# Three moves in a hand-written TensorE order: second gate row behind the first row's copies, first row later, state products one step behind the turned keys

## The chip, the cores and the metric

The kernel runs on one core of a Trainium2 chip, as one program in one launch. The metric is the device time of one execution in microseconds (us); less is better. The runs of one kernel differ by some tenths of a per cent, so a difference under about 0.5% of the time isn't told apart from none.

## What is computed

One inference step of a small diffusion backbone: 128 context tokens and 512 latent tokens (T = 640 together), width 1,024, two layers. Layer 0 (even) has four HGRN2 heads (state 128 x 128) and four GLA heads (state 64 x 128) that share one input projection; layer 1 (odd) has eight retention heads. Each head is a chunkwise gated linear scan in both directions:

```python
def even_mixer(h, s0_a, s0_b, lb, w_in, gk_w, gk_b, gn_w, w_out):
    p = h @ w_in
    aq, ai, af_f, af_b, ag, bq, bk, bv, bg, bl_f, bl_b = jnp.split(p, EVEN_SPLIT_IDX, axis=-1)
    ...
    o_a, st_a = bidir_scan(hd(jax.nn.silu(aq), H_A), (-jnp.expm1(lf_f), -jnp.expm1(lf_b)),
                           hd(ai, H_A), (lf_f, lf_b), s0_a)
    def gla_log_gate(low, d):
        return jax.nn.log_sigmoid((low @ gk_w[d] + gk_b[d]).astype(jnp.float32)) / GLA_GATE_NORM
    ...
    o = group_rms_norm(o, gn_w).astype(h.dtype) * jax.nn.silu(jnp.concatenate([ag, bg], axis=-1))
    return o @ w_out, st_a, st_b

# chunk_gated_linear, per direction:  S_t = diag(g_t) S_{t-1} + k_t v_t^T,  o_t = S_t^T q_t
```

Conditioning: shift, scale and gate of a layer are `SiLU(c) @ ada_w[l] + ada_b[l]`. The outputs are the normed tokens of both groups and the scan states of the context tokens.

## The kernel before, in words

**Matmuls.** Each float32 weight tile (128 x 512, 256 KB, loaded by SyncE in L171) is split in two parts: `wh` (a cast on ScalarE, L180) and the remainder `wl` (a subtraction on GpSimd, some on VectorE, L182). The activations are split likewise (`h0h`, `h0l`, `h1h`, `h1l` by token group; the groups are 256 and 384 columns). A projection with features on the partitions (`proj_fm`, PSUM tiles `pf`) has 8 steps over the 1,024 inputs ("k-steps") of 6 matmuls each, 48 in all; with tokens on the partitions (`proj_tm`) the tiles are called `pt`. The trace shows each of the small fp32 matmuls (`px`, `pkv`, `po`, `pada`, `pz`) as two records, so 16 matmuls of `pada` are "x32". All PSUM tiles share eight buffers in turn: a matmul that begins a new tile waits for whoever read the tile that had the buffer before.

**The order of TensorE is written by hand.** `run(gen)` walks through a projection, and after each k-step it looks whether the work in the queue `bg` is due by a clock that the program advances by estimated matmul lengths; if so, it lets that generator go on to its next `yield d`, which makes it due again `d` later. `low_bg` is a second queue: `ada_stream`, the conditioning of layer 0's gate and of layer 1, in 16 steps of 16 `pada` matmuls, each on four `araw` tiles of 256 KB (L281, four buffers in all, loaded by SyncE once the matmuls of the step before have freed them). `drain(left)` steps `bg` with no projection in between until `left` generators remain; while the one in front isn't due, it steps `low_bg` instead. The other engines' order (VectorE = DVE, ScalarE = ACT, GpSimd = POOL, SyncE = SP) follows from a scheduler of the framework; each engine runs its own list in order.

**GLA's rows.** The four GLA heads are two rows of two heads. `gla_gates(r)` (L746 to L767) makes a row's gates `T1` (in the code `g1`): 4 matmuls `pz`, absolute value (L755), ACT table loads, Exp and Ln (L757, L758), `T1 <- T1 - e` (L759, DVE), Exp (L762), Ln (L764), and on DVE L765 and L767. For each row the loop (L774 on) projects the queries (`use_bq`, copied by ACT, L779) and the keys (`use_bk`: one copy by DVE, L783, one by ACT, L784), multiplies Q = q x gate on POOL (`prepare`, L656 and L657) and puts the row's generator in `bg`.

**A row** (`row`, L659 on) computes the scores on the diagonal (`px` from q and K), then six levels, each: `kmix` (ACT, L687) gathers `km`, 20 matmuls `px` from Q and km, `merge` on DVE: K x gates (L695), Q x gates (L697), and the next level's gates (L699, half as long at each level); the scores are copied into A (L706, L714, L716 to L718). Then it turns the keys: 8 transposes `pkt` and two ACT copies `kt` (L725), `yield D_KT`; then the products `pkv` and the states S (DVE, L405 and L408), `yield D_KV`; then the outputs `po` (first v x A, then S x Q).

**HGRN's heads** (loop behind it): project q, `drain(1)` (the head before the last must be finished), project the two forget gates, then K (L819), T1 (L821), `ks` (POOL) and `prepare`, and the row goes into `bg` with a delay of 7.0. Behind the heads stand the decays of layer 1 and the gate projections (`pt`), which the last rows share.

Of the kernel before, what the change touches and what calls it, by code (L numbers as in the profile page):

```python
# [41 lines left out]
def hybrid_kernel(  # L42
# [20 lines left out]
    def ps(name="ps"):  # L63
        return psp.tile([128, 512], F32, tag="ps", name=name)

    def tokt(name):
        return tok.tile([128, D], F32, tag="tok", name=name)

    def t25(name):
        return misc.tile([128, T], F32, tag="t25", name=name, bufs=3)  # L70
# [9 lines left out]
    def mm(out, lhsT, rhs, share=1, **kw):  # L80
        n = 1
        for _, cnt in rhs.ap[1:]:
            n *= cnt
        clock[0] += (max(n, 256) / 2400.0 if lhsT.dtype == F32R else max(n, 128) / 600.0) / share
        PE.matmul(out, lhsT, rhs, **kw)  # L85
# [5 lines left out]
    def add_bg(gen, delay=0.0, queue=bg):  # L91
        queue.append([gen, clock[0] + delay])

    def step(queue):
        e, late = queue[0], len(deferred) if queue is bg else 0
        try:
            wait = next(e[0])
            e[1] = clock[0] + wait
        except StopIteration:
            queue.pop(0)  # L100
            return
        flush(late)
# [5 lines left out]
    def run(gen):  # L108
        for _ in gen:
            while bg and bg[0][1] <= clock[0]:  # L110
                step(bg)
            if low_bg and low_bg[0][1] <= clock[0]:
                step(low_bg)
# [60 lines left out]
    def weights(i, look=None):  # L174
        while made[0] <= min(i + (LOOK if look is None else look), len(specs) - 1):
            n = made[0]
            src = specs[n]
            raw, _ = raw_load(src)
            wh = wp.tile([128, 512], F32R, tag="wh", name="wh", bufs=8)
            S.copy(wh, raw)  # L180
            wl = wp.tile([128, 512], F32R, tag="wl", name="wl", bufs=8)
            (V if n in on_dve else G).tensor_tensor(wl, raw, wh.bitcast(F32), op=SUB)  # L182
            loaded[n] = tuple(w.rearrange("p (a b) -> p a b", a=src.shape[1]) for w in (wh, wl))
            made[0] += 1
        return loaded[i]
# [23 lines left out]
    def in_turn(sums, first, last):  # L209

        for n in range(3):
            for out, pairs in sums:
                mm(out, *pairs[n], start=first and n == 0, stop=last and n == 2)

    def proj_fm(ids, act, use):
        p = [ps("pf") for _ in GROUPS]
        for k in range(KC):
            wh, wl = (w[:, k % 4, :] for w in weights(ids[k // 4]))
            sums = []
            for g in (1, 0):  # L220
                hh, hl = (a[:, k, :] for a in act[g])
                sums.append((p[g][:, :GROUPS[g][1]], ((wh, hh), (wh, hl), (wl, hh))))
            in_turn(sums, k == 0, k == KC - 1)
            if k < 7:
                yield
        for g in (1, 0):
            use(g, p[g])
        yield
# [265 lines left out]
    def x_square(t):  # L494
        return rms(x_t[t], junk)
# [19 lines left out]
    with tc.manual_schedule(engines={mybir.EngineType.Activation, mybir.EngineType.DVE, mybir.EngineType.Pool}):  # L515
# [8 lines left out]
        r = [x_square(t) for t in range(2)]  # L524
# [129 lines left out]
    def prepare(Q, q, g1):  # L654

        G.tensor_tensor(Q[:, 0, :], q, g1[:, 0, :], op=MUL)  # L656
        G.tensor_tensor(Q[:, 1, :], q, g1[:, 1, :], op=MUL)  # L657
# [76 lines left out]
    def new_KQ():  # L734
        return tuple(rows.tile([128, 2, T], F32, tag=n, name=n, bufs=2) for n in "KQ")

    def new_q():
        return rows.tile([128, T], F32, tag="q", name="q", bufs=2)

    def new_g():  # L740
        return rows.tile([128, 2, T], F32, tag="T1", name="T1", bufs=2)
# [4 lines left out]
    def gla_gates(r):  # L746

        K, Q, q, g1 = gla[r]
        e = Q
        for d in range(2):  # L750
            b = vecs[:, O_GKB + 2 * d + r:O_GKB + 2 * d + r + 1]
            for g, (off, n) in enumerate(GROUPS):
                p = ps("pz")
                mm(p[:, :n], gkw[:, d, 128 * r:128 * r + 128], low[:, off:off + n], start=True, stop=True)
                S.activation(e[:, d, off:off + n], p[:, :n], AF.Abs, bias=b)  # L755
                V.tensor_scalar(g1[:, d, off:off + n], p[:, :n], b, 0.0, op0=ADD, op1=ALU.min)
        S.activation(e, e, AF.Exp, scale=-1.0)  # L757
        S.activation(e, e, AF.Ln, bias=1.0)  # L758
        V.tensor_tensor(g1, g1, e, op=SUB)  # L759
        y0 = [t25("y0") for d in range(2)]  # L760
        for d in range(2):
            S.activation(y0[d], g1[:, d, :], AF.Exp, scale=1.0 / 16.0)  # L762
        for d in range(2):
            S.activation(e[:, d, :], y0[d], AF.Ln, bias=tiny)  # L764
        V.scalar_tensor_tensor(e, g1, 1.0 / 16.0, e, op0=MUL, op1=SUB)  # L765
        for d in range(2):
            V.scalar_tensor_tensor(g1[:, d, :], e[:, d, :], 1.0, y0[d], op0=ADD, op1=MUL)  # L767

    gla_gates(0)
    gla_gates(1)  # L770
    y_t = [tokt(f"y{t}") for t in range(NT)]
    gn = tokt("gn")
    ACTQ.dma_start(gn, gn_even[0:1, :].to_broadcast([128, D]))
    for r in range(2):  # L774
        K, Q, q, g1 = gla[r]

        def use_bq(g, p, q=q):
            off, n = GROUPS[g]
            S.activation(q[:, off:off + n], p[:, :n], AF.Copy, scale=0.125)  # L779

        def use_bk(g, p, K=K):
            off, n = GROUPS[g]
            V.tensor_copy(K[:, 0, off:off + n], p[:, :n])  # L783
            S.copy(K[:, 1, off:off + n], p[:, :n])  # L784

        run(proj_fm(ids_b[r][0], act, use_bq))
        run(proj_fm(ids_b[r][1], act, use_bk))
        prepare(Q, q, g1)
        s0 = [state_gla[0, 0, d, 2 * r:2 * r + 2].rearrange("h k v -> (h k) v") for d in range(2)]
        cols = [512 + 256 * r, 640 + 256 * r]  # L790
        add_bg(row(q, g1, K, Q, (K[:, 0, :], 2.0), [(0, 64), (64, 128)], cols, cols, s0,
                   new_gla[0, 0, :, 2 * r:2 * r + 2].rearrange("d h k v -> (h k) d v"), y_t, gn), D_GLA)


    def v_use(t, p):
# [3 lines left out]
    for h in range(4):  # L799
        q = new_q()  # L800
# [7 lines left out]
        g1 = new_g()  # L808
# [9 lines left out]
        K, Q = new_KQ()  # L818
# [194 lines left out]
    for part in range(2):  # L1013
        p = ps("pt")
        for k in range(KC):
            wh, wl = weights(ids_o1[1][k])
            cols = slice(256 * part, 256 * part + 256)
# [3 lines left out]


DVE_FROM = 5
D_LEVEL, D_KT, D_KV, D_GLA, D_PREP, D_ROPE, D_TURN, D_ADA, D_RT, D_RV = 1.8, 0.5, 1.2, 7.0, 7.0, 11.0, 2.5, 7.0, 1.5, 1.5


# [42 lines left out]
```

## Time and profile before

| | before |
|---|---|
| runs | 795.43 us median of 3 (794.3 to 798.55) |
| the profiled execution | 797.16 us, span 795.4 us, granted clock 0.984 |
| TensorE (PE) | 758.2 us busy, 95% of the span |
| DVE, ACT, POOL | 428.8, 334.2 and 289.6 us busy (54%, 42%, 36%) |
| HBM | 86.31 MB read, 8.16 MB written, 119 GB/s over the span |

TensorE is the engine that is nearly always busy; the others have room on average, and matter where TensorE waits for one of them. The granted clock is given as a share of 2.4 GHz. Times within the program are microseconds from the start of the span. GLA's rows lie between 62 and 165 us, HGRN's heads between 165 and 335, and behind 390 us the rest of the program stands in the same order as after the change.

### The profile page before, as it was taken

How to read it: one execution, taken by the hardware profiler on the slowest of the kernel's cores; microseconds unless marked ns; L12 is line 12 of the kernel's file. 1: busy time of each engine (PE TensorE's matmuls, PEld its weight loads, DVE VectorE, ACT ScalarE, POOL GpSimd, SP SyncE). 2: the span in 40 equal slices, each digit the busy share in tenths (PEclk: the TensorE clock that was granted, in tenths of full speed). 3: DMA queues.
4: the chain of work that ended last, by engine and by line, in shares of the span. 5: the costliest groups of instructions: out<-in, count | busy, mean ns of one | idle time of the engine just before them, and what ended most of it. 6: DMA issues, size and time to landing. Idle time of an engine off the chain costs nothing.

```text
span 795.4 us, 15429 instructions
## 1 busy us (share of the span) xinstructions
PE 758.2 (95%) x6116; PEld 664.2 (84%) x6116; DVE 428.8 (54%) x744; ACT 334.2 (42%) x757; POOL 289.6 (36%) x263
## 2 busy tenths in 40 slices
PE   4999789999989899899999999999999999999996
PEld 3768778789889798778888888899999999888885
DVE  4973793752986666663444940036454646324433
ACT  6447643444534444443534552324333332235322
POOL 2261430265552522331344521544443532043221
PEclk9999899999999999999999999999999999999998
DMA  9982432364433431318524432334333333544003
GB/s 292 315 268 92 142 108 62 114 181 126 144 96 107 147 98 38 81 41 265 152 84 145 152 118 87 94 105 106 100 104 90 115 91 94 173 126 133 14 26 133
DMA packets 104776, 98.62 MB, mean 124 GB/s; under 512 B 7660, under 2 KB 80896, under 8 KB 104704
## 3 DMA queue, kind: packets, MB, share of 16 engines
q1 hardware_dynamic: 83520, 82.15, 33.4%
q10 hardware_dynamic: 21184, 15.49, 7.1%
q8 instruction: 48, 0.79, 0.4%
q14 instruction: 24, 0.20, 0.1%
HBM read 86.31 MB, written 8.16 MB: 119 GB/s over the span
## 4 chain that ended last, share of the span: by engine, by line
PE 68%; DVE 8%; issue 2%; ACT 1%; POOL 1%; DMA 1%; ACTq 0%; POOLq 0%; DVEq 0%
PE pt L85 32%; PE pf L85 21%; PE po L85 5%; PE px L85 4%; PE pkv L85 3%; DVE K L695 2%; DVE T L821 1%; DVE T L699 1%; PE pyt L89 1%; PE pada L85 1%; PE pkt L89 1%; DMA rot<-qk 1%; DVE K L819 1%; DVE Q L697 1%; PE pxt L89 1%
## 5 line engine op out<-in xcount | busy, mean ns | idle before, releaser
L182 POOL TENSOR_TENSOR wl<-raw,wh 128x512 fp32r<-128x512 f32 x142 | 203.0, 1444 | 309.4 <-ACT wh L180 264.4
L180 ACT CAST wh<-raw 128x512 fp32r<-128x512 f32 x168 | 103.2, 621 | 97.8 <-PE pf L85 37.0
L85 PE MATMUL pf<-h0h,wh 128*128 128x384 f32 (+1 forms) x256 | 64.1, 332 | 0.0
L335 DVE SCALAR_TENSOR_TENSOR y<-po,rr,gn 128x128 f32<-128x128 f32 x80 | 24.2, 345 | 72.3 <-POOL rr L158 60.5
L85 PE MATMUL pf<-h1h,wh 128*128 128x384 f32 (+1 forms) x256 | 60.3, 317 | 0.0
L85 PE MATMUL pf<-h0l,wh 128*128 128x384 f32 (+1 forms) x256 | 58.9, 311 | 0.0
L85 PE MATMUL pf<-h0h,wl 128*128 128x384 f32 (+1 forms) x256 | 58.6, 310 | 0.0
L85 PE MATMUL pf<-h1l,wh 128*128 128x384 f32 (+1 forms) x256 | 58.3, 309 | 0.0
L85 PE MATMUL pf<-h1h,wl 128*128 128x384 f32 (+1 forms) x256 | 58.3, 309 | 0.0
L687 ACT COPY km<-K 128x640 f32<-128x640 f32 x42 | 32.8, 782 | 56.3 <-DVE K L695 40.8
L85 PE MATMUL pt<-wh,h1h 128*128 128x512 f32 x160 | 53.9, 402 | 0.0
L156 POOL TENSOR_SCALAR rv<-ss 128x3 f32<-128x3 f32 (+1 forms) x32 | 11.0, 345 | 113.0 <-ACT junk L327 111.8
L85 PE MATMUL pt<-wh,h1l 128*128 128x512 f32 x160 | 52.1, 390 | 0.0
L85 PE MATMUL pt<-wl,h1h 128*128 128x512 f32 x160 | 52.0, 390 | 0.0
L697 DVE TENSOR_TENSOR Q<-Q,T 128x640 f32<-128x640 f32 x42 | 40.5, 964 | 19.2 <-PE px L85 19.1
L916 DVE TENSOR_TENSOR qk<-qk,cs 128x1024 f32<-128x1024 f32 x8 | 9.8, 1226 | 74.9 <-DMA rot<-qk 74.9
L695 DVE TENSOR_TENSOR K<-K,T 128x640 f32<-128x640 f32 x42 | 44.8, 1067 | 6.4 <-ACT km L687 5.9
L327 ACT ACTIVATE junk<-po 128x128 f32<-128x128 f32 x80 | 22.3, 278 | 54.0 <-PE po L85 41.7
L85 PEld LDWEIGHTS pf<-h0h,wh 128*128 128x128 f32 x256 | 39.6, 192 | 4.8 <-issue 2.3
L85 PE MATMUL pt<-wh,h0h 128*128 128x512 f32 x120 | 43.7, 429 | 0.0
L85 PEld LDWEIGHTS px<-Q,km 64*64 64x64 f32 (+1 forms) x1120 | 29.9, 139 | 15.7 <-issue 9.7
L85 PE MATMUL px<-Q,km 64*64 64x64 f32 (+1 forms) x1120 | 35.6, 231 | 5.9 <-DVE Q L697 4.8
(219 smaller groups left out, 1702.2 us busy)
## 6 DMA issues: line engine op xcount, KB each, us to landing
raw<-in_w_in_even_dram SPq DMA_DIRECT2D x64, 256.0 KB, 3.0
araw<-in_ada_w_dram SPq DMA_DIRECT2D x64, 256.0 KB, 3.7
raw<-in_w_in_odd_dram SPq DMA_DIRECT2D x64, 256.0 KB, 2.9
ada<-in_ada_w_dram SPq DMA_DIRECT2D x16, 512.0 KB, 6.3
raw<-in_w_out_even_dram SPq DMA_DIRECT2D x24, 256.0 KB, 3.0
rot<-qk ACTq DMA_DIRECT2D x32, 128.0 KB, 3.5
raw<-in_w_out_odd_dram SPq DMA_DIRECT2D x16, 256.0 KB, 3.0
x<-xr SPq DMA_DIRECT2D x5, 512.0 KB, 2.7
```

What stands on the lines that cost most here:

```text
L85: PE.matmul(out, lhsT, rhs, **kw)
L89: PE.transpose(out, in_, ident[0:in_.shape[0], 0:in_.shape[0]])
L156: G.tensor_scalar(v[:, :n], ssum, 1.0 / count, EPS, op0=MUL, op1=ADD)
L180: S.copy(wh, raw)
L182: (V if n in on_dve else G).tensor_tensor(wl, raw, wh.bitcast(F32), op=SUB)
L327: S.activation(junk, p[:, 128 * i:128 * i + 128], AF.Square, accum_out=ss[:, j:j + 1])
L335: V.scalar_tensor_tensor(dst, p[:, 128 * i:128 * i + 128], r[:, j:j + 1], dst if have else gn[:, col:col + 128], op0=MUL, op1=MUL)
L687: S.copy(km.rearrange("p (n b h) -> p n b h", b=2, h=h), ap(kf, 0, ([2 * h, T // (2 * h)], [T + h, 2], [1, h])))
L695: V.tensor_tensor(keys, keys, ap(th, 1, ([nn - 1, 2], [2, nb], [0, h])), op=MUL)
L697: V.tensor_tensor(queries, queries, ap(th, 0, ([nn + 1, 2], [2, nb], [0, h])), op=MUL)
L699: V.tensor_tensor(t2, ap(th, 0, ([nn, 2], [2, nb])), ap(th, 1, ([nn, 2], [2, nb])), op=MUL)
L916: V.tensor_tensor(lat, lat, cos.unsqueeze(1).to_broadcast([128, 2, 512]), op=MUL)
```

## The change

It moves three things and adds no operation. (1) `gla_gates(1)` is no longer called with `gla_gates(0)` but in the loop, behind the first row's two projections and its `prepare`. (2) The first row's generator is put in `bg` behind the second row's query projection, due at once, where before it was put there behind the first row's projections, due 7.0 later. (3) `D_KT`, the time between the transposes of the keys and the products `pkv`, is 3.0 instead of 0.5, in all six rows of layer 0.

```diff
     gla_gates(0)
-    gla_gates(1)
...
         run(proj_fm(ids_b[r][0], act, use_bq))
+        if r:
+            add_bg(first_row, 0.0)
         run(proj_fm(ids_b[r][1], act, use_bk))
         prepare(Q, q, g1)
...
-        add_bg(row(q, g1, K, Q, (K[:, 0, :], 2.0), [(0, 64), (64, 128)], cols, cols, s0,
-                   new_gla[0, 0, :, 2 * r:2 * r + 2].rearrange("d h k v -> (h k) d v"), y_t, gn), D_GLA)
+        this_row = row(q, g1, K, Q, (K[:, 0, :], 2.0), [(0, 64), (64, 128)], cols, cols, s0,
+                       new_gla[0, 0, :, 2 * r:2 * r + 2].rearrange("d h k v -> (h k) d v"), y_t, gn)
+        if r:
+            add_bg(this_row, D_GLA)
+        else:
+            first_row = this_row
+            gla_gates(1)
...
-D_LEVEL, D_KT, D_KV, D_GLA, D_PREP, D_ROPE, D_TURN, D_ADA, D_RT, D_RV = 1.8, 0.5, 1.2, 7.0, 7.0, 11.0, 2.5, 7.0, 1.5, 1.5
+D_LEVEL, D_KT, D_KV, D_GLA, D_PREP, D_ROPE, D_TURN, D_ADA, D_RT, D_RV = 1.8, 3.0, 1.2, 7.0, 7.0, 11.0, 2.5, 7.0, 1.5, 1.5
```

**What it moves on DVE, at GLA's first row.** T_770 are row 0's gates, T_774 row 1's; the tiles made from T_770 by L699 are the gates of the following levels; y_794 and y_795 are row 0's. The order before:

```order
L765 SCALAR_TENSOR_TENSOR Q<-T_770,Q 128x1280
L759 TENSOR_TENSOR T_774<-T_774,Q 128x1280
L767 SCALAR_TENSOR_TENSOR T_770<-Q,y_794 128x640
L767 SCALAR_TENSOR_TENSOR T_770<-Q,y_795 128x640
L699 TENSOR_TENSOR T_1148<-T_770 128x640
L699 TENSOR_TENSOR T_1208<-T_1148 128x320
L699 TENSOR_TENSOR T_1262<-T_1208 128x160
L699 TENSOR_TENSOR T_1332<-T_1262 128x80
L765 SCALAR_TENSOR_TENSOR Q<-T_774,Q 128x1280
L783 COPY K<-pf 128x384
```

and in the changed kernel (L782 is the key copy there):

```order
L765 SCALAR_TENSOR_TENSOR Q<-T_770,Q 128x1280
L767 SCALAR_TENSOR_TENSOR T_770<-Q,y_794 128x640
L767 SCALAR_TENSOR_TENSOR T_770<-Q,y_795 128x640
L699 TENSOR_TENSOR T_1162<-T_770 128x640
L699 TENSOR_TENSOR T_1214<-T_1162 128x320
L699 TENSOR_TENSOR T_1268<-T_1214 128x160
L699 TENSOR_TENSOR T_1348<-T_1268 128x80
L699 TENSOR_TENSOR T_1402<-T_1348 128x40
L699 TENSOR_TENSOR T_1462<-T_1402 128x20
L699 TENSOR_TENSOR T_1516<-T_1462 128x10
L782 COPY K<-pf 128x384
L782 COPY K<-pf 128x256
```

Row 1's L759 and L765 have left the stretch, the last three L699 stand ahead of the copies instead of behind them, and both copies of K follow the whole of row 0's gates. Row 1's L759, L765 and L767 come behind the copies, ahead of row 0's first L695.

**What it moves on ACT, at the same place.** In the changed kernel (L783 is ACT's key copy there, y_994 and y_995 are row 1's):

```order
L755 ACTIVATE Q<-pz,vecs 128x384
L757 ACT_TABLE_LOAD
L757 ACTIVATE Q<-Q 128x1280
L758 ACT_TABLE_LOAD
L758 ACTIVATE Q<-Q 128x1280
L259 COPY arow<-pada 128x128
L180 CAST wh<-raw 128x512
L762 ACT_TABLE_LOAD
L762 ACTIVATE y_994<-T_774 128x640
...
L764 ACTIVATE Q<-y_995,tiny 128x640
L687 COPY km<-K 128x640
```

Before, the first `km` stood right behind the two key copies; now three of row 1's four L755 and the rest of its gates stand between. On TensorE row 1's four `pz` stand behind the first row's key projection, and the second matmul of the next projection begins a PSUM tile whose buffer ACT's 384-column key copy frees. The first scores stand one k-step later than before.

**What it moves on TensorE, at HGRN's head 0.** v_753 to v_755 are value tiles, A the scores, S the states. The order before:

```order
L85 MATMUL pkv<-v_755,kt 128x128
L85 MATMUL pada<-araw,condp 32x128 x16
L85 MATMUL pf<-h0h_113,wh 128x384
...
L85 MATMUL po<-v_753,A 128x128
L85 MATMUL po<-v_754,A 128x128
L85 MATMUL po<-v_755,A 128x128
L85 MATMUL po<-S,Q 128x128 x6
L85 MATMUL pf<-h0h_113,wh 128x384
```

and in the changed kernel:

```order
L85 MATMUL pkv<-v_755,kt 128x128
L85 MATMUL pada<-araw,condp 32x128 x32
L85 MATMUL po<-v_753,A 128x128
L85 MATMUL po<-v_754,A 128x128
L85 MATMUL po<-v_755,A 128x128
L85 MATMUL po<-S,Q 128x128 x6
L89 MATMUL padv<-ident,arow 128x128
L85 MATMUL pada<-araw,condp 32x128 x16
L85 MATMUL po<-v_751,A 128x128
L85 MATMUL po<-v_752,A 128x128
L85 MATMUL po<-S,Q 128x128 x2
L85 MATMUL pada<-araw,condp 32x128 x16
```

Before, `pkv` stood six `pf` behind `pkt`, and one k-step or more stood between any two of the pieces; now it stands 18 `pf` behind, so late that `drain(1)` of head 2 does the rest of the row, with four steps of `low_bg` in it and no `pf`. At head 1 `pkv` stands 12 `pf` behind `pkt` (before six), and `po` directly behind `pkv` in the drain of head 3 (before 12 `pf` between). At heads 2 and 3, 18 `pt` stand between `pkt` and `pkv` instead of six.

## Rows read from the trace of the kernel before

**Rows 1.** The page: busy time by engine; the chain that ended last, by engine.
```profile
PE 758.2 (95%) x6116; PEld 664.2 (84%) x6116; DVE 428.8 (54%) x744; ACT 334.2 (42%) x757; POOL 289.6 (36%) x263
...
PE 68%; DVE 8%; issue 2%; ACT 1%; POOL 1%; DMA 1%; ACTq 0%; POOLq 0%; DVEq 0%
```

**Rows 2.** Windows: stretch, length, busy PE PEld DVE ACT POOL, PEclk, DMA share, GB/s.
```profile
92.00:115.00 23.00, 15.34 (x284) 13.63 (x283) 19.92 (x27) 9.14 (x17) 7.63 (x5) 0.85 0.40 123
...
238.00:240.00 2.00, 2.00 (x21) 1.74 (x23) 1.90 (x5) 0.00 (x0) 0.07 (x1) 0.53 0.36 102
```

**Rows 3.** Timeline, PE, GLA's start: start, duration, engine, line, tiles, count [idle before].
```profile
63.85 4.81 PE L85 MATMUL pz<-low,gkw 128*128 128x256 f32 x16
68.21 0.74 PE L85 MATMUL pf<-h0h,wh 128*128 128x384 f32 x2
...
95.14 0.92 PE L85 MATMUL px<-q,K 64*64 64x64 f32 x24 [2.94 <-DVE K L783]
```

**Rows 4.** Timeline, ACT, the gates of both GLA rows.
```profile
65.47 2.02 ACT L755 ACTIVATE Q<-pz,vecs 128x384 f32<-128x384 f32 x4 [0.41 <-PE pz L85]
67.51 1.28 ACT L757 ACT_TABLE_LOAD   x1
68.81 1.28 ACT L757 ACTIVATE Q<-Q 128x1280 f32<-128x1280 f32 x1
...
79.62 1.55 ACT L764 ACTIVATE Q<-y,tiny 128x640 f32<-128x640 f32 x2
```

**Rows 5.** Timeline, DVE, the same stretch and the first level behind it.
```profile
81.21 1.49 DVE L765 SCALAR_TENSOR_TENSOR Q<-T,Q 128x1280 f32<-128x1280 f32 x1 [5.63 <-ACT Q L764]
...
84.02 2.65 DVE L767 SCALAR_TENSOR_TENSOR T<-Q,y 128x640 f32<-128x640 f32 x2
86.71 6.41 DVE L699 TENSOR_TENSOR T<-T 128x640 f32<-128x640 f32 x4
...
94.44 0.55 DVE L783 COPY K<-pf 128x384 f32<-128x384 f32 x1
...
100.74 2.17 DVE L695 TENSOR_TENSOR K<-K,T 128x640 f32<-128x640 f32 x1
```

**Rows 6.** Timeline, POOL, at DVE's four L699.
```profile
86.02 2.07 POOL L656 TENSOR_TENSOR Q<-q,T 128x640 f32<-128x640 f32 x1 [0.76 <-DVE T L767]
```

**Rows 7.** Timeline, PE, HGRN's heads.
```profile
206.95 1.08 PE L85 MATMUL pada<-araw,condp 128*32 128x128 f32 x32
...
210.98 0.83 PE L85 MATMUL px<-Q,km 128*64 128x64 f32 x20 [0.99 <-DVE Q L697]
...
236.85 2.65 PE L85 MATMUL pkv<-v,kt 128*128 128x128 f32 x16 [2.20 <-ACT kt L725]
239.43 1.94 PE L85 MATMUL pada<-araw,condp 128*32 128x128 f32 x32
...
243.05 1.50 PE L85 MATMUL po<-S,Q 128*128 128x128 f32 x12
...
278.40 3.18 PE L85 MATMUL pkv<-v,kt 128*128 128x128 f32 x16 [2.15 <-ACT kt L725]
...
319.91 1.95 PE L85 MATMUL pkv<-v,kt 128*128 128x128 f32 x16
...
324.69 0.49 PE L85 MATMUL po<-S,Q 128*128 128x128 f32 x2 [0.79 <-DVE S L405]
326.71 2.38 PE L85 MATMUL po<-S,Q 128*128 128x128 f32 x10 [1.53 <-DVE S L408]
```

**Rows 8.** Timeline, DVE, head 2: L699 over 640 columns at another place.
```profile
319.32 0.81 DVE L699 TENSOR_TENSOR T<-T 128x640 f32<-128x640 f32 x1
```

**Rows 9.** Timeline, DVE, head 1's states (L408 follows, as many).
```profile
281.69 1.11 DVE L405 SCALAR_TENSOR_TENSOR S<-S,T,pkv 128x128 f32<-128x128 f32 x3
```

**Rows 10.** The tile `araw`: SP's issues (ns, min/median/max), and issue to landing.
```profile
L281 SPq DMA_DIRECT2D araw<-in_ada_w_dram x64: 328/389/1722, 46.2 to 291.6; - x64
...
DMA to landing us min/median/max: 2.7/3.7/5.4
```

## The prediction

> **What bounds the kernel now.** I read the page first, then the windows, then TensorE's timeline for its idle stretches, and for each of those the engine that ended it. TensorE (PE) is busy 95% of the span and makes up 68% of the chain that ended last; VectorE (DVE) has 8% [rows 1]. So the time is PE's work plus PE's waits, and the change adds and removes no work: it can only move waits. PE idles at few places. The largest lies from 92 to 115 us, where PE works 15.34 of 23.00 us, so 7.66 us idle, at a granted clock of 0.85 [rows 2]; its first wait is 2.94 us for K's copy on DVE [rows 3]. Then come one wait in head 0, two for the turned keys (`kt`), and two for the states [rows 7]. After an idle stretch PE runs slower: a granted clock of 0.53 from 238 us, the 1.2 GHz level of its two, after the wait of 2.20 us [rows 2, 7]. The forecast asks which of these waits goes, and which is late next.
>
> **Term A, the first GLA row (66 to 115 us).** Eight `pz` matmuls take the 4.4 us from 63.85 to 68.21 [rows 3]; the second row's four go behind the first row's projections, so these begin about 2.2 us earlier, at 66.0. Row 0's gate chain loses what row 1 had put between on ACT (three L755 at 2.02/4, one pass of about 1.3), some 2.5 us [rows 4]: L765 starts at 78.7 instead of 81.21, and, since row 1's L759 no longer stands behind it, L767 at 80.2 instead of 84.02 [rows 5]. From L767's start to the fourth L699's end the trace has 9.1 us (84.02 to 93.12) [rows 5]; three L699 of 40 columns and fewer add an estimated 0.6: 89.9.
>
> In DVE's new order both copies of K stand behind all of this. With 0.55 for DVE's copy and as much for ACT's [rows 5], K's first accumulator is free at about 90.9. The second matmul of the next projection takes the PSUM buffer that ACT copy frees. PE gets there early: from 68.21 to 92.20 it did three projections and two `pada` steps of 1.08 [rows 3, 7], 7.3 us each projection; so 66.0 + 2 x 7.3 + 1.1 + 2.2 (`pz`) = 83.9. **It waits 7.0 us** where before it waited 2.94 at the scores.
>
> Behind that copy ACT now has row 1's gates ahead of `km`: three L755 (1.5), four table loads (4 x 1.28), passes over 1,280 columns (2 x 1.28, 2 x 1.55 at most) [rows 4], and a cast, two small copies and `km` itself, estimated at 1.9 together: 14.2 us, ready at 105.1. PE needs 7.3 + 1.1 + 0.9 + 0.9 with about 0.6 for the lower clock, and is there at 101.7: **3.4 us**. Level 2 needs, behind ACT's last pass (104.1), L765 1.49, L767 2.65, L695 at up to 2.17 [rows 5], and a weight remainder and L697, estimated together at 2: 112.4, against PE at 109.4: **3.0 us**. With 0.8 for the levels after, 14.2 us against 7.66: **+6.5**. Bounds: 90.9 rests on L699's four taking 6.41 us while POOL multiplies Q in 2.07 us [rows 5, 6]; the same 640-column L699 takes 0.81 elsewhere [rows 8]. At that pace all four are under 2.5 us and A is about +1; with every operation behind L767 as slow as the slowest row, +9. I take the upper row, since L656 and L657 are still released by the same L767.
>
> The Trainium skill ("SBUF — State Buffer", "Who interferes with whom") says that a VectorE instruction with two SBUF inputs and a GpSimd instruction that reads SBUF exclude each other for a whole instruction, and that one with a single SBUF input outside some modes does not. By that rule the 6.41 stays as long as POOL's order stays, and A is +6.5; read without it, from the 0.81 alone, A would be +1.
>
> **Term C, head 0.** PE waits 0.99 for L697 [rows 7]. The row now begins one k-step of projection (0.9) earlier in the PE order and the `pada` step ahead of that level (1.08) lies elsewhere: up to 2.95. I take 2.7, **+1.7** (0 to 2).
>
> **Terms D and G, the later products.** `pkv` of head 0 waited 2.20 for `kt`, ran 2.65 instead of 1.95, and the `pada` step behind it 1.94 instead of 1.08 [rows 7]. It now stands 18 `pf` instead of 6 behind its transposes, and later in all: the wait goes, **-3.7**. Head 1: 2.15, and 3.18 instead of 1.95 [rows 7], and an estimated 0.5 on the matmuls behind it: **-3.9**. This is what the change buys. If `kt` gets later still, half of it comes back.
>
> **Term E, the drain at head 2.** With `pkv` later, head 0's row is not finished when the program drains it ahead of head 2's forget gates. There nothing fills: the PE order has `pkv`, two ada steps, `po`, an ada step, `po`, an ada step. Before, these steps lay one at a time among `pf`. A step empties the four `araw` buffers, and the next one's tiles are only then asked for: 0.39 us for an issue, 3.7 for landing [rows 10]. First tile free at 1.95 + 0.27 = 2.2 us after the start; three refills of 4.1 + 0.27 make 13.1, the last three tiles follow 0.39 apart: 16.5 us in all. PE's work in it is 1.95 + 4 x 1.08 + 26 `po` at 1.50/12 less overlap, about 3.0 [rows 7]: 9.3. So 7.2 idle, and about 1.6 for the clock after it, what D showed (0.70 + 0.86): **+8.8**. With landings of 2.7 or 5.4 [rows 10], +5.8 or +13.9; the middle is taken because loads here come in fours, as everywhere. SP has a weight load ahead of them, which waits for POOL: for the upper end.
>
> The Trainium skill ("DMA: Bandwidth & Descriptors", "Where the ~2 µs actually goes") puts a fixed cost of about 2 us on a transfer, most of it completion. The trace's 3.7 us at 256 KB is above that; with the page's figure alone E would be up to 5.1 us smaller.
>
> **Term H, the drain at head 3.** Head 1's `pkv` is followed at once by `po`, with nothing of a projection between. `po` on S needs the states: L405 x3 1.11 and L408 as much [rows 9], less the 0.7 of `po` on A: 1.5 at least; DVE also gets to L405 late, behind the merge (2.9). **+3.2** with the clock (+1.5 to +4).
>
> **Term J, head 2.** The waits for the states, 0.79 and 1.53 [rows 7], shrink as `pkv` moves 12 `pt` back, but the states move too: **-0.7** (-2.3 to +1).
>
> GLA's own products had no wait before; the later place costs nothing while 18 `pt` cover the states' 2.2 us; without them H's 1.5 would come in. From the second layer on the order is the same.
>
> **Sum.** 6.5 + 1.7 - 3.7 + 8.8 - 3.9 + 3.2 - 0.7 = +11.9 us. The profiled execution took 797.16 us (span 795.4); that gives 809.1. The median of the runs shown, 795.43, lies 1.7 lower: **807.3 us**. About 0.5%, 4 us, is what a measurement of this kernel can tell from no change.
>
> **Rivals.**
> *VectorE runs unhindered* (not slower). If, with row 1's gates out of the way, DVE's two-input operations no longer meet POOL's, all terms bound by DVE fall: A +1, C 0, H +0.5, J -2.3; D, E, G stay: +0.4, **about 796 us**. It decides where row 0's four long L699 stand: under 3 us in all, this; over 5, my forecast. For it: 0.81 for the same shape [rows 8]. Against: 6.41 at this place, and L656 released there as before [rows 5, 6]. Chance 0.17; in a quarter of that the refills are also at the short end (another 3.0), and it is faster.
>
> *The refills are long.* Landings of 5.4 (+5.1) and A at +9 (+2.5): **815 us**. For it: twelve `araw` loads in a row, with a weight load ahead; against: 3.7 as the median of 64 such loads [rows 10]. Chance 0.12.
>
> *The drain costs little* (E at half, because ACT and DVE run ahead meanwhile and H falls with it): 807.3 - 4.4 - 2 = **801**. That is inside the forecast's case.
>
> *The change doesn't do what it says.* It speaks of a projection; in PE's order the first scores move by only six `pf` (0.9 us), as the old due time of 7.0 had nearly the same effect. So no gain from that part is counted; if the order were all that mattered and no wait moved, **795 us**; chance 0.05, with a little of it on the faster side.
>
> **Chances.** Forecast with its bounds (800 to 812) 0.66, unhindered 0.17, long refills 0.12, nothing moves 0.05. Faster 0.07, no difference 0.15, slower 0.78. The range takes in the unhindered case's middle and the long one's: 796 to 816.
>
> **What would show it.** Right: PE waits some 7 us about 84 us for ACT's copy of K, and 3 us for `km` near 102; no wait at head 0's and head 1's `pkv`; ahead of head 2's gates four `pada` steps with three waits of 2 to 3 us on `araw`; a wait on L405/L408 between head 1's `pkv` and `po`. Wrong: K's copy by 86 us, `araw` landing before PE asks, or `pkv` still waiting for `kt`.

## The result, and the profile after

The changed kernel takes 826.39 us (median of 4 runs, 823.13 to 827.5) against 795.82 us for the kernel before (4 runs, 794.3 to 798.55): a ratio of 1.0387, interval 1.0361 to 1.0412. The direction was forecast; 807.3 us, and a range up to 816, were not enough. The loss is 30.6 us, not 12.

The page of the changed kernel, busy time and the chain, answers to [rows 1]:

```profile
PE 767.4 (93%) x6116; PEld 668.4 (81%) x6116; DVE 431.6 (52%) x746; ACT 337.6 (41%) x759; POOL 288.2 (35%) x263
...
PE 75%; DVE 13%; issue 4%; DMA 3%; ACT 2%; POOL 2%; ACTq 0%; SPq 0%; POOLq 0%; DVEq 0%
```

The instructions of TensorE are as many as before, yet it is busy 9.2 us longer. Most of that is the lower clock, which takes 15.7 us of the changed kernel against 8.7 before (summed from windows, as below). DVE and DMA have risen in the chain, and the waits show for what. TensorE's timeline (start, duration, engine, line, tiles, count, [idle before]) shows each of them; first GLA's rows and the first head:

```profile
90.00 0.58 PE L85 MATMUL pf<-h0h,wh 128*128 128x256 f32 x1 [6.83 <-ACT K L783]
...
104.06 1.05 PE L85 MATMUL px<-Q,km 64*64 64x64 f32 x40 [1.81 <-issue]
...
112.19 1.35 PE L85 MATMUL px<-Q,km 64*64 64x64 f32 x40 [2.65 <-DVE Q L697]
...
166.29 0.81 PE L85 MATMUL px<-Q,km 64*64 64x64 f32 x40 [0.71 <-DVE Q L697]
...
171.19 0.81 PE L85 MATMUL px<-Q,km 64*64 64x64 f32 x40 [1.62 <-DVE Q L697]
...
183.34 0.43 PE L85 MATMUL pada<-araw,condp 128*32 128x128 f32 x8 [2.41 <-DMA araw<-in_ada_w_dram]
...
225.46 0.82 PE L85 MATMUL px<-Q,km 128*64 128x64 f32 x20 [2.26 <-DVE ab L266]
```

In two of these rows the name behind the arrow doesn't say what TensorE waited for. The 1.81 us at 104.06 end 0.10 us after ACT's first `km` of row 0 (102.96 + 1.00), and the 2.26 us at 225.46 belong to L697, as in the kernel before: L266 is a small operation that ended just behind it (DVE's timeline).

```profile
224.49 0.83 DVE L697 TENSOR_TENSOR Q<-Q,T 128x640 f32<-128x640 f32 x1 [0.26 <-issue]
225.23 0.16 DVE L266 TENSOR_TENSOR ab<-padv,vecs 128x8 f32<-128x8 f32 x1
```

Then come the two drains and the end of layer 0. Here [rows 7] had the waits for `kt` and the states:

```profile
252.98 2.05 PE L85 MATMUL pkv<-v,kt 128*128 128x128 f32 x16 [0.16 <-ACT kt L725]
...
259.78 0.65 PE L85 MATMUL pada<-araw,condp 128*32 128x128 f32 x8 [3.74 <-DMA araw<-in_ada_w_dram]
...
270.72 0.43 PE L85 MATMUL pada<-araw,condp 128*32 128x128 f32 x8 [1.80 <-DMA araw<-in_ada_w_dram]
...
304.79 2.05 PE L85 MATMUL pkv<-v,kt 128*128 128x128 f32 x16 [0.15 <-ACT kt L725]
...
310.82 0.80 PE L85 MATMUL po<-S,Q 128*128 128x128 f32 x2 [3.31 <-DVE S L405]
...
383.17 0.80 PE L85 MATMUL px<-Q,km 128*64 128x64 f32 x20 [2.40 <-DVE Q L697]
...
408.80 0.33 PE L89 MATMUL pyt<-ident,y 128*128 128x128 f32 x1 [3.74 <-DVE y L354]
```

To see what all this costs I cut both traces into windows of 2 us and took from each the idle time (2 less PE's busy time) and what the lower clock took (busy time x (1 - PEclk)). Two such windows of the changed kernel, in the drain ahead of head 2 (columns as in [rows 2]):

```profile
260.00:262.00 2.00, 1.09 (x16) 0.20 (x8) 0.34 (x2) 0.27 (x1) 0.00 (x0) 0.50 0.83 270
262.00:264.00 2.00, 1.99 (x19) 1.17 (x20) 0.00 (x0) 0.27 (x1) 0.00 (x0) 0.50 0.88 284
```

The first has 0.91 us idle and loses 0.55 to the clock; the second loses 1.0 to the clock though TensorE never stops. Summed by place (us, idle + clock; the letters are the prediction's terms):

| place | before | after | difference | forecast |
|---|---|---|---|---|
| A: GLA's start | 7.7 + 2.3 | 11.3 + 5.8 | +7.1 | +6.5 |
| GLA row 1 | 0.7 + 0 | 5.2 + 1.7 | +6.2 | none |
| C: head 0's first levels | 1.0 + 0 | 2.3 + 0 | +1.3 | +1.7 |
| D: head 0's `pkv` | 2.2 + 1.7 | 0.2 + 0 | -3.7 | -3.7 |
| E: drain ahead of head 2 | - | 7.6 + 3.9 | +11.5 | +8.8 |
| G: head 1's `pkv`, and `px` behind it | 2.5 + 1.6 | 0.2 + 0 | -3.9 | -3.9 |
| H: drain ahead of head 3 | - | 3.9 + 2.8 | +6.7 | +3.2 |
| J: head 2's states | 2.3 + 1.5 | 0 | -3.8 | -0.7 |
| head 3, wait for L697 | - | 2.4 + 0 | +2.4 | none |
| the y transposes | - | 3.8 + 1.5 | +5.3 | none |

These places sum to +29.1 us, of 30.1 between the two spans. Beside them a dip of the clock ahead of 62 us, which of the two executions only the one before shows, takes off 1.6, the part behind 434 us adds 0.6, and some 2 us of TensorE's busy time stand at no place. Before the runs, the theory was this ledger: each loss belongs to the move that stands at its place. The rival was that the losses hang on the phase, on where a row's steps fall against loads and weight remainders, so that the moves' costs don't add.

### The profile page after: what moved, and what is told of

The parts are those of the page before. It is cut to its first block, busy times and chain, and to the rows that moved or that the text cites. A ratio compares the mean times of both kernels' runs of the same rounds, so it can differ in the third digit from the quotient of the medians.

```text
span 825.5 us, 15431 instructions
## 1 busy us (share of the span) xinstructions
PE 767.4 (93%) x6116; PEld 668.4 (81%) x6116; DVE 431.6 (52%) x746; ACT 337.6 (41%) x759; POOL 288.2 (35%) x263
## 4 chain that ended last, share of the span: by engine, by line
PE 75%; DVE 13%; issue 4%; DMA 3%; ACT 2%; POOL 2%; ACTq 0%; SPq 0%; POOLq 0%; DVEq 0%
PE pt L85 31%; PE pf L85 24%; PE po L85 6%; PE px L85 4%; PE pkv L85 2%; PE pada L85 2%; DVE T L699 2%; DMA araw<-in_ada_w_dram 2%; PE pbv L85 2%; DVE K L695 2%; DVE Q L697 2%; PE pyt L89 1%; POOL wl L182 1%; PE pkt L89 1%; PE pxt L89 1%
## 5 line engine op out<-in xcount | busy, mean ns | idle before, releaser
L182 POOL TENSOR_TENSOR wl<-raw,wh 128x512 fp32r<-128x512 f32 x142 | 204.6, 1455 | 301.5 <-ACT wh L180 265.3
L85 PE MATMUL pf<-h0h,wh 128*128 128x384 f32 (+1 forms) x256 | 66.2, 340 | 6.8 <-ACT K L783 6.8
L697 DVE TENSOR_TENSOR Q<-Q,T 128x640 f32<-128x640 f32 x42 | 44.0, 1048 | 24.6 <-PE px L85 24.1
L695 DVE TENSOR_TENSOR K<-K,T 128x640 f32<-128x640 f32 x42 | 44.4, 1058 | 7.9 <-ACT km L687 7.2
```

The lines of the kernel that those rows point to most:

```text
L695: V.tensor_tensor(keys, keys, ap(th, 1, ([nn - 1, 2], [2, nb], [0, h])), op=MUL)
L697: V.tensor_tensor(queries, queries, ap(th, 0, ([nn + 1, 2], [2, nb], [0, h])), op=MUL)
```

## The experiments

### One move at a time (three kernels) and the drain without its ada steps

First only the gates' move (the call of `gla_gates(1)` behind the first row's `prepare`), only the first row's (`add_bg(first_row, 0.0)`), and only the constant:

```diff
-D_LEVEL, D_KT, ... = 1.8, 0.5, ...
+D_LEVEL, D_KT, ... = 1.8, 3.0, ...
```

> Of the change only the first move: row 1's gates behind the first row's copies. Ledger theory (each loss of the changed kernel belongs to the move that stands at its place): TensorE waits 6 to 7 us for ACT's copy of K and some 2 to 4 us for km and L697 behind it, against 7.7 us of idle before; nothing changes at the heads: 801 to 804 us. Rival (the losses come from the lag, which shifts every later step against the loads): the first row's lag of 6 to 7 us brings most of the later waits too: over 812 us.

> Of the change only the second move: the first row's generator asked for behind the second row's query projection. In TensorE's order its first scores stand one k-step (six pf) later. Ledger theory: the 2.94 us wait for K's copy is shorter by up to 0.9 us, row 1's levels keep their waits: 794 to 797 us, no difference from before. Rival (the move shifts row 1 onto GpSimd's run of weight remainders): 798 to 801 us.

> Of the change only the third move: D_KT 3.0. Ledger theory: the kt waits at heads 0 and 1 and the states' wait at head 2 go (7 to 11 us gained), the two drains cost 11.6 and 6.7 us, row 1 behind its later products 4 to 6, and the end of layer 0, with 24 pt instead of 48 between the last po and the y transposes, 5 to 8: 813 to 820 us. Rival (row 1's and the end's losses belong to the lag of the gates): 799 to 806 us.

Measured, against 794.38 us for the kernel before on that chip (in brackets the ratio and its interval): gates 812.69 (1.0213, 1.0171 to 1.0254), first row 800.88 (1.0070, 1.0043 to 1.0098), D_KT 821.04 (1.0323, 1.0284 to 1.0363). **The costs don't add**: 18 + 6.5 + 27 = 51.5 us apart, 31 together. The ledger was 1 us too low for D_KT, and wrong for the other two. At GLA's start the gates' move cost what it costs in the whole change (the wait for K 6.80 us, then 4.44 for `km`); the other 10 us lie elsewhere: two waits for `araw` at row 1 and at 307 us, and more at the heads. The first row's move, one k-step, cost nothing at its place, and row 1's waits stayed as they were (0.70 us for L697), so the rival's number came true and its cause did not. What head 0 had waited for at `kt` it now waited for at the states (TensorE's timeline):

```profile
233.80 1.61 PE L85 MATMUL pkv<-v,kt 128*128 128x128 f32 x13
235.35 1.08 PE L85 MATMUL pada<-araw,condp 128*32 128x128 f32 x32
237.34 0.83 PE L85 MATMUL po<-v,A 128*128 128x128 f32 x6
...
241.24 0.80 PE L85 MATMUL po<-S,Q 128*128 128x128 f32 x2 [3.06 <-DVE S L405]
```

Here `pkv` came without a wait, with D_KT still 0.5 and six `pf` behind `pkt` as before, and the 3 us stood behind it. ACT's timeline says why. In the kernel before, the two copies to `kt` stand behind a `km` of the next head, which waits for DVE's L695:

```profile
234.87 0.79 ACT L687 COPY km<-K 128x640 f32<-128x640 f32 x1 [3.37 <-DVE K L695]
...
236.21 1.07 ACT L725 COPY kt<-pkt 128x512 f32<-128x512 f32 x2
```

With the first row's move they stand ahead of it:

```profile
232.71 1.07 ACT L725 COPY kt<-pkt 128x512 f32<-128x512 f32 x2
236.28 0.81 ACT L687 COPY km<-K 128x640 f32<-128x640 f32 x1 [2.50 <-DVE K L695]
```

In both kernels DVE's L695 and L699 of the next head stand ahead of L405, which makes the states. So the waits at `kt` and at the states are one lateness, DVE's, and ACT's order decides at which of the two it shows. A later `pkv` is no gain unless work of TensorE fills the time ahead of `po` as well.

Fourth, the changed kernel with the ada stream left out of this drain:

```diff
-            if queue is bg and low_bg and queue[0][1] > clock[0]:
+            if low and queue is bg and low_bg and queue[0][1] > clock[0]:
...
-        drain(1)
+        drain(1, low=False)
```

> The changed kernel, but the drain ahead of heads 2 and 3 no longer steps the ada stream while the row isn't due; the ada steps lie among pf again. Ledger theory: the three refills of araw (7.6 us idle, 4.0 us of lower clock) go, and a wait on the states as at head 3 (about 4 us idle, 2 to 3 us of clock) takes their place: 819 to 823 us. Rival (the refills only stood where the states would have been waited for, or the reverse: the ada steps were not the cost): within 2 us of 826.

It takes 811.44 us (1.0195, 1.0160 to 1.0231), 15 us less than the changed kernel, where at most 7 were expected. In the drain ahead of head 2 the refills are gone and the wait for S that they had covered shows (2.73 us for L405, 0.62 for L408; with the clock 6.1 us against 11.5). Most of the other 10 us came elsewhere: the ada steps stood among `pf` at head 1 and in head 3's drain 4.2 us were lost instead of 6.7, 30 `pt` instead of 24 stood ahead of the y transposes (a wait of 0.70 us instead of 3.74), and the wait for L697 at head 3 was 0.93 instead of 2.40. So the refills were dearer than their own stretch.

### Where the copies of K stand

The changed kernel, and in the same way the kernel before and the first two moves alone, with the first row's copies of K both on ACT:

```diff
-            V.tensor_copy(K[:, 0, off:off + n], p[:, :n])
+            if r:
+                V.tensor_copy(K[:, 0, off:off + n], p[:, :n])
+            else:
+                S.copy(K[:, 0, off:off + n], p[:, :n])
             S.copy(K[:, 1, off:off + n], p[:, :n])
```

> The changed kernel, but the first row's two copies of K both on ACT, so that none stands behind row 0's gates on DVE. Theory (the wait at the second row's query projection is for a copy that stands in DVE's order behind the seven L699): the wait of 6.83 us falls to 1 us or less, and about half of it comes back as a longer wait for km, which still stands behind row 1's gates on ACT; 820 to 824 us. Rival (the wait is TensorE's for the gates themselves, by whatever copy): the sum of the waits before 116 us stays at 11.3 us, 825 to 828 us.

> The first two moves without D_KT. Theory (the first moves cost 7 us at GLA's start, and what each single move added later came from the phase of the rows against the loads, which is another one here): the ada step at row 1 waits for no araw, every po keeps matmuls of a projection between it and pkv: 803 to 809 us. Rival (the moves' costs add): 812.7 + 6.5, about 819 us.

> The first two moves, D_KT 0.5, and the first row's two copies of K on ACT. Theory (what the first two moves cost at GLA's start is the copy's place in DVE's order): 7 us less than the two moves alone, 801 to 804 us, the rest at the heads. Rival (row 1's gates ahead of km on ACT are the cost): 806 to 810 us.

The changed kernel with the copies moved takes 817.33 us (1.0285, 1.0265 to 1.0305), 9 us less than with them on DVE and below the expected band. The wait at the query projection is gone, and some 4 us of it come back behind the first scores, as the theory had it (TensorE's timeline):

```profile
98.79 1.34 PE L85 MATMUL px<-Q,km 64*64 64x64 f32 x40 [5.18 <-issue]
...
106.93 0.84 PE L85 MATMUL px<-Q,km 64*64 64x64 f32 x40 [3.04 <-DVE Q L697]
```

But the clock falls only once there, so that GLA's start loses 10.2 us (8.8 idle, 1.4 of clock), about as in the kernel before; that is 7 of the 9 us. The first two moves alone took 809.32 us (1.0186, 1.0168 to 1.0204), with no wait for `araw` at row 1, a little above the theory's band and far from the sum of the single moves. With the copies on ACT they took 800.88 (1.0065, 1.0046 to 1.0084), as much as the first row's move alone. So what the gates' move costs at its place is the copies' place in DVE's order, not row 1's gates on ACT.

### Whose later products cost what

`D_KT` 3.0 for some rows only, told apart by the row's heads or columns, for example:

```diff
-        yield D_KT
+        yield 3.0 if vcol == [512, 640] else D_KT
```

> D_KT 3.0 for the four HGRN heads alone, all else as before. Theory (the drains and the end of layer 0 are the heads' cost, the waits for L697 and araw at row 1 are the GLA rows'): no new wait before 235 us; the drains ahead of heads 2 and 3 and the end as in the third move alone, less 6 to 8 us for row 1: 811 to 816 us. Rival (row 1's waits are independent of its own D_KT): 818 to 823 us.

> D_KT 3.0 for the two GLA rows alone. Theory (row 1's later products cost the araw wait behind GpSimd-bound weight loads; the other part of what GLA's D_KT costs, some 8 us, is a third refill in the drain ahead of head 2, which needs the heads' D_KT too): 802 to 806 us. Rival (GLA's rows cost 16 to 17 us by themselves, the difference between D_KT in all rows and in the heads alone): 810 to 813 us.

> D_KT 3.0 for GLA's row 0 alone, all else as before. Theory (row 1's waits come from row 0: its later products put row 1's levels and the ada step behind them further behind the start of the pf weights' loads and remainders, and the araw loads stand behind those on SP): the wait for araw near 175 us, 4 us and 3 to 4 of lower clock, is there in full: 801 to 805 us. Rival (it comes from row 1's own later products): no wait for araw there, 795 to 798 us.

The four heads alone took 804.44 us (1.0139, 1.0106 to 1.0172), far below the band expected. Both GLA rows alone took 804.16 (1.0097, 1.0081 to 1.0113), within theirs; GLA's row 0 alone 807.48 (1.0162, 1.0142 to 1.0182), above its band and more than both rows together. Heads and GLA rows are +9 and +8, all six +27; so the later products don't add either, and row 1's took off some of what row 0's cost. For the heads alone three ada steps lie in the drain ahead of head 2, not four; TensorE's timeline of that kernel:

```profile
241.06 0.42 PE L85 MATMUL pada<-araw,condp 128*32 128x128 f32 x8 [1.53 <-DMA araw<-in_ada_w_dram]
...
251.49 0.43 PE L85 MATMUL pada<-araw,condp 128*32 128x128 f32 x8 [1.22 <-DMA araw<-in_ada_w_dram]
```

The drain loses 6.6 us of idle and clock there, where the constant in all rows had 9.0 + 6.1 = 15.1: most of the 9 us that don't add. GLA's rows shift the ada stream, and with it the number of its steps that fall into the drain. For the wait at row 1, row 0's later products suffice. SyncE's and TensorE's timelines of the kernel with row 0 alone:

```profile
156.57 12.67 SPq L171 DMA_DIRECT2D raw<-in_w_in_even_dram  x8
169.29 3.08 SPq L281 DMA_DIRECT2D araw<-in_ada_w_dram  x4
```

```profile
173.53 1.31 PE L85 MATMUL pada<-araw,condp 128*32 128x128 f32 x16 [4.32 <-DMA araw<-in_ada_w_dram]
```

SyncE issues in order, and ahead of the four `araw` loads stand eight weight loads that take 12.67 us, since each waits for a buffer that GpSimd frees with a weight remainder (nine in a row there, 14.87 us; SyncE's waits name L182 eight times). The ada step before had ended at 162.93, so the `araw` buffers were free 6.4 us before their loads were issued. In the kernel before, the loads for the second of two ada steps there were issued 7.0 us ahead of it (SyncE's and TensorE's timelines):

```profile
170.35 2.04 SPq L281 DMA_DIRECT2D araw<-in_ada_w_dram  x4
```

```profile
166.77 1.08 PE L85 MATMUL pada<-araw,condp 128*32 128x128 f32 x32
...
177.36 1.08 PE L85 MATMUL pada<-araw,condp 128*32 128x128 f32 x32
```

In the changed kernel the two steps began at 173.01 and 180.50, and the issue was 4.2 us ahead of the second:

```profile
176.27 2.04 SPq L281 DMA_DIRECT2D araw<-in_ada_w_dram  x4
```

More buffers for `araw`, or another queue for its loads, weren't tried. In the changed kernel DVE's L697 at row 1 takes 1.92 and 1.56 us instead of 0.81 while GpSimd works on that run of remainders; there stand the waits of 0.71 and 1.62.

### The end of layer 0

The changed kernel with D_KT 0.5 at head 3 alone:

```diff
-        yield D_KT
+        yield 0.5 if vcol == [384] else D_KT
```

> The changed kernel, but D_KT 0.5 again at HGRN's head 3 alone, the last row of layer 0: 36 pt instead of 24 stand between its last po and the y transposes. Theory (the wait at the y transposes, 3.75 us and 1.5 of lower clock, is the y of head 3's last tokens, with 12 pt, some 2.8 us, too few between): it falls to 1 us or none, the wait for L697 at this head stays: 820 to 823 us. Rival (that wait comes from DVE's and ACT's work there, wherever the outputs stand): 825 to 828 us.

TensorE's timeline there:

```profile
408.51 0.33 PE L89 MATMUL pyt<-ident,y 128*128 128x128 f32 x1 [0.25 <-DVE y L354]
```

The wait of 3.74 is 0.25, the wait for L697 stays (2.39): the 12 missing `pt` it was. The median is 824.07 us (1.0367, 1.0348 to 1.0385), 2.3 below the changed kernel; the two intervals overlap, so the trace shows this cause and the median doesn't. It is less than the 5.3 at the place; in the profiled execution dips of the clock stood elsewhere (1.5 us at the first head's first levels, 1.7 at L697, none in the changed kernel).

### Can it be beaten?

Two tries on the waits for `kt` and the first scores, on the kernel before. One makes the heads' K on ACT:

```diff
-        V.tensor_scalar(K, g1,
-                        nclb[:, h:h + 1], clb[:, h:h + 1], op0=MUL, op1=ADD)
+        S.activation(K, g1, AF.Identity, scale=nclb[:, h:h + 1], bias=clb[:, h:h + 1])
```

> The kernel before, D_KT 0.5, but K <- nclb*T1 + clb of the HGRN heads (1.4 us each on DVE) made by ACT. Theory (the wait for kt is set by the next head's first operations, which stand ahead of this head's merge, kt copies and states on DVE and ACT; the time between pkt and pkv only chooses whether kt or S is waited for): each kt wait falls by about 1.4 us, some of the lower clock goes with it: 788 to 793 us. Rival (kt waits for ACT, which has the K operation now): no gain, 793 to 799 us.

It takes 795.92 us (1.0001, 0.9984 to 1.0018), no gain. The theory of what `kt` waits for was not tested by it, for the chain kept its length: ACT's K, then DVE's T1 (timelines of the two engines in that kernel).

```profile
227.05 1.46 ACT L819 ACTIVATE K<-T,clb,nclb 128x1280 f32<-128x1280 f32 x1
```

```profile
228.54 2.30 DVE L820 TENSOR_SCALAR T<-T,clb,lbv 128x1280 f32<-128x1280 f32 x1 [1.93 <-ACT K L819]
```

L820 overwrites the T1 that K is read from, so DVE waited 1.93 us for ACT where it had worked 1.40 itself; the wait for `kt` stayed at 2.26.

> The kernel before with one edit: the first GLA row's two copies of K both on ACT. Theory (the first scores wait for DVE's copy behind DVE's gate operations): the waits of 2.94 and 0.88 us before the first scores go or shrink to 1 us together, part comes back at km and L697, which wait for DVE; 791.5 to 794 us. Rival (L697 on DVE sets the second level whatever the first scores do): no difference, 794 to 796 us.

> A candidate from the runs so far: the kernel before, the first row's copies of K on ACT, and D_KT 1.3 for HGRN's head 2 alone, whose products lie among pt with no drain behind. Theory: the waits for the states at head 2 (2.3 us idle, 1.5 of lower clock) go, 42 pt remain ahead of the y transposes and no wait comes there; 787 to 791 us. Rival (the later row meets the weight remainders at head 3's levels and a wait for L697 of 2.4 us with 1.7 of clock comes, as with D_KT 3.0): 792 to 795 us.

The edits are the copies of K as above, and `yield 1.3 if vcol == [256] else D_KT` for head 2. With the copies of K on ACT: 793.13 us (0.9957, 0.9940 to 0.9973); with D_KT 1.3 at head 2 besides: 791.97 (0.9955, 0.9936 to 0.9973). Both intervals lie below 1, but 0.4% is under the 0.5% that count here as a difference; it is a hint and no more, and the second edit adds nothing that can be told. At head 2 the waits for the states fell from 2.3 to 1.25 us and did not go, and a wait of 0.92 us for L697 came at head 3. With the copies of K alone, the waits ahead of the scores are gone and a single longer one is left, for DVE's L697 at the next level (TensorE's timeline):

```profile
104.49 1.35 PE L85 MATMUL px<-Q,km 64*64 64x64 f32 x40 [6.02 <-DVE Q L697]
```

## Why the prediction failed

**Right by their steps.** Term A's steps on DVE were right almost row by row. DVE and ACT of the changed kernel:

```profile
77.91 1.49 DVE L765 SCALAR_TENSOR_TENSOR Q<-T,Q 128x1280 f32<-128x1280 f32 x1 [4.30 <-ACT Q L764]
79.44 2.54 DVE L767 SCALAR_TENSOR_TENSOR T<-Q,y 128x640 f32<-128x640 f32 x2
82.01 6.96 DVE L699 TENSOR_TENSOR T<-T 128x640 f32<-128x640 f32 x7
88.88 0.88 DVE L782 COPY K<-pf 128x384 f32<-128x384 f32 x2
```

```profile
89.47 0.75 ACT L783 COPY K<-pf 128x384 f32<-128x384 f32 x2 [7.67 <-DVE K L782]
...
102.96 1.00 ACT L687 COPY km<-K 128x640 f32<-128x640 f32 x1
```

Forecast 78.7 for L765, 80.2 for L767, 90.9 for K's copy; measured 77.9, 79.4 and 89.9. POOL's L656 again fell on the long L699 (81.32 to 83.37), and all seven took 6.96 us, so the rival "VectorE runs unhindered" is out and the upper row was the right one to take. The rule of the Trainium skill ("SBUF — State Buffer", "Who interferes with whom") pointed the right way.

**Right by luck.** The size of A, +7.1 against +6.5, hides two errors that cancel. Its waits were 6.83, 1.81 and 2.65 us, where 7.0, 3.4, 3.0 and 0.8 were forecast: TensorE's idle time rose by 3.6 us, not 6.5, above all since `km` was there at 104.0 instead of 105.1 and TensorE half a microsecond later. The lower clock added 3.5 us (5.8 against 2.3). The term left that out, but for 0.6 in TensorE's arrival: it set idle time against idle time. Nor was it an accident of this execution: in four other kernels with this wait for K (the gates' move alone, the first two moves, the drain without ada steps, head 3 early) the lower clock took 4.7 to 7.0 us there. In E the refills' idle time, 7.6 us against 7.2, came out too, but `po` hid the middle one of the three and the other two were longer (4.7 and 2.9 us). Landings had a median of 3.6 us and a maximum of 6.6 here; the fixed cost of about 2 us that "DMA: Bandwidth & Descriptors" of the Trainium skill gives for loads issued through GpSimd ("Where the ~2 µs actually goes") would by itself have been too low for these, which SyncE issues.

C, D and G came out within 0.5 us. (At head 0 `pkv` stands 24 `pf` behind its transposes, not 18, and in C only the earlier start counts: six `pf` took the place of the `pada` step.)

**The step that failed** is the sentence "GLA's own products had no wait before; the later place costs nothing while 18 `pt` cover the states' 2.2 us". It looked for a wait at the moved instruction alone, and there indeed none came. But a later end of row 0 is a later start of row 1, whose steps then meet the weight loads and remainders otherwise: +6.2 us at row 1. The first two moves without D_KT have no wait for `araw` there, the whole change has, and row 0's D_KT alone suffices. It is not the only way to that wait: the gates' move alone has it as well. The same shift sets which ada steps fall due in the drain; the order listing had shown that result, and E counted it.

**The end of layer 0** had no term: "From the second layer on the order is the same" is true and beside the point, since what is in the same order can wait for what comes ahead of it. 24 `pt` instead of 48 stood between the last `po` and the y transposes, as TensorE's order has it, and the last y was not ready: +5.3 us; with 36 the wait was 0.25 us. The wait for L697 at head 3, +2.4, was not seen either. In DVE's timeline of the changed kernel L697 stands behind a weight remainder that waits for ACT's cast:

```profile
380.46 1.31 DVE L182 TENSOR_TENSOR wl<-raw,wh 128x512 fp32r<-128x512 f32 x1 [2.89 <-ACT wh L180]
...
382.30 0.81 DVE L697 TENSOR_TENSOR Q<-Q,T 128x640 f32<-128x640 f32 x1
```

It came in all five kernels with D_KT 3.0 at head 2 and the ada steps in the drain (2.4 us), one of which had head 3's D_KT at 0.5, and with 0.93 us in the one whose drain had no ada steps. Head 2 is the cause as far as the runs go: D_KT 1.3 there, the only difference to a kernel without this wait, brought 0.92 us, again behind such a remainder (it waited 2.31 us for the cast). TensorE's timeline of that kernel:

```profile
351.16 0.80 PE L85 MATMUL px<-Q,km 128*64 128x64 f32 x20 [0.92 <-DVE Q L697]
```

D_KT 3.0 at head 2 alone was not tried.

**Mis-sized terms.** The clock in E: 1.6 forecast, 3.9 measured. H: 3.2 forecast, 6.7 measured (idle 3.9 where I had 2.9, clock 2.8 where I had 0.3). J: -0.7 forecast, -3.8 measured, in the change's favour.

Of the difference to the forecast, 18 us, the places without a term make 13.9 and the mis-sized ones, E, H and J together, 3.1; A adds 0.6, C takes off 0.4, and the other 1 us lies outside the table.

## What to carry to other kernels

A later due time moves the step, what stands behind it in the queue, and every transfer that a filler step triggers; cost it at each of these places, up to the next point where all engines meet, and not at the wait it was made for. Where a wait is one engine's lateness, it can show under another name, as it did at `kt` and S here: look whether the time gained is filled. A copy that frees an accumulator is part of TensorE's path, so ask what stands ahead of it in its engine's order; putting it on an engine that was idle there was worth 9 us in the changed kernel, though no more than a hint of a gain in the kernel before.

## What was not expected of the hardware

The same wait cost two different prices. Head 0's 2.20 us ahead of `pkv` was followed by matmuls at a granted clock of 0.53 in the kernel before [rows 2, 7], the lower level, and by the full clock in the kernel with the copies of K on ACT, whose instructions at this place are the same (windows of that kernel):

```profile
236.00:238.00 2.00, 0.99 (x8) 0.99 (x9) 1.90 (x2) 1.42 (x3) 1.92 (x2) 1.00 0.00 0
238.00:240.00 2.00, 2.00 (x42) 1.68 (x40) 1.90 (x5) 0.00 (x0) 0.22 (x1) 1.00 0.28 66
```

The difference is 1.7 us at this place alone. So the price of the clock behind a short wait, taken from one execution, was one of two values here, and a sum should carry both. And the size of a DVE operation says little where POOL works: of the three L699 over 40, 20 and 10 columns, which took 0.61 us together before, two took 2.98 us in that kernel, while POOL ran L656 and L657 (DVE's timeline):

```profile
98.89 2.98 DVE L699 TENSOR_TENSOR T<-T 128x20 f32<-128x20 f32 x2
```
